# Split weights kept in device memory, the scan's chunks chained, and the rotary's GpSimd work moved, in a two-layer decoder trunk

## The chip, the cores and the metric

One core of a Trainium2 chip runs the whole kernel. The metric is the device time of one execution in microseconds (us); three runs of the kernel before gave a median of 2995.03 us (2994.13 to 2998.02). A core has five engines that run side by side: PE (matrix multiply, with PEld for its weight loads), DVE (VectorE), ACT (ScalarE), POOL (GpSimd) and SP (SyncE), which here issues the DMAs. Each engine takes its instructions in order. Tiles live in SBUF (128 partitions) and, for results of PE, in the banks of PSUM; tensors too large for that live in device memory (DRAM).

## What is computed

2048 tokens of width 1024, with 16 learned meta tokens ahead of them (2064 in all), pass two layers in float32. Each layer is h + norm(mixer(norm(h))).

```
layer 0:  q, k, v, g_a, glu_in, g_b = split(h @ w_in)            # 1024 -> 2816 = 22 blocks of 128
          a = sliding_window_attention(rope(q), rope(k), v, sinks) * silu(g_a)   # 8 heads, window 128, meta tokens always seen
          u = glu_in[:512] * sigmoid(glu_in[512:])
          c = silu(layer_norm(depthwise_conv31(u))) @ w_pw2 * silu(g_b)
          y = concat(a, c) @ w_out
layer 1:  q, k, v, g = split(h @ w_in)                            # 1024 -> 4096, 16 heads of 64
          z = q k^T / 8                                           # only keys before the query
          a = sigmoid(z) * product of sigmoid(-z) over the keys between it and the query   # stick-breaking, no softmax
          y = ((a @ v) * silu(g)) @ w_out
rope(x):  (x1 * cos - x2 * sin, x2 * cos + x1 * sin) on the two halves of a head
```

## The kernel before

*Precision.* PE multiplies in a reduced float format (`F32R`). To keep float32 accuracy, most operands are split into a high part (the value rounded to that format) and a low part (the rest), and a product is made of three matmuls, high x high, low x high and high x low (`mm3`, L126 to L130).

*Layer 0, first stage* (`stage1`, L251). The tokens are cut into 4 chunks (528 tokens, then three of 512). For a chunk, the normalised and transposed input stands in SBUF as a high and a low tile. `proj(m, ...)` (L277) multiplies it with block `m` of the 22 blocks of `w_in`: `weights` (L112) loads 512 KB by DMA into `raw` (two buffers), ACT casts it to the high part `wh` (L119) and POOL subtracts to get the low part `wl` (L120). Both parts have two buffers each, in a pool that the pointwise convolution's weights use too. The load carries a priority that lets the planner put it 60 instructions ahead. All 22 blocks are loaded and split again in each of the four chunks. The projections feed the rotary embedding (`rope`, L329: five per chunk), values, gates and the gated convolution input.

*The rotary.* ACT copies a projection out of PSUM (`qr`), four small DMAs make a copy with the halves exchanged (`qs`). Some time later, after the next projection (`turn`, L337 to L344), DVE multiplies `qr` by the cosines, POOL `qs` by the signed sines, DVE adds, POOL rounds to the high part and POOL subtracts for the low part; DMAs store both.

*The convolution* has 31 taps on DVE, one `scalar_tensor_tensor` of 128x512 each (L294), queued in the background and issued six at a time after projections. *The second stage* of layer 0 (`stage2`: attention over the window, layer norm, the pointwise product `pw` at L524, which loads and splits two weight blocks for each pair of token tiles) is interleaved with the first stage of the next chunk. The softmax's meta columns are copied by POOL into `pmc` (L447). The output projection of layer 0 runs into the start of layer 1.

*Layer 1.* For each of 8 pairs of heads, and in two halves of the queries, the projections of the next pair (`proj` at L736) are interleaved with attention (`attn`, L822). There, `chunk` (L882) works on two blocks of 128 queries, two heads, and up to 512 keys, from the latest keys back: PE makes the scores `z`, ACT makes `om` = sigmoid(-z) and `be` = sigmoid(z) from them (L902, L903), and on the diagonal POOL puts 1 and 0 where the key isn't before the query (L906). DVE then runs a product scan over `om` from the last key to the first (L910), started with the product of all chunks before it, and multiplies `be` with the scan's value one place on (L913). The product so far passes from chunk to chunk through POOL: it copies the scan's first column to `carry` (L912) and, for the next chunk, `carry` into the column behind the scan (L909); the first chunk has a 1 there (L907). PE transposes `be` (L930), ACT copies it out (L936), and PE multiplies it with the values (L944).

*Order.* The order of the instructions on each engine, and on SP's DMA queue, is made by a planner that simulates a timeline from the written order, priorities and its own costs; waits between engines are semaphores that it sets. A tile's buffer is given out anew when all that used it are through.

Of the kernel before, what the change touches and what calls it, by code (L numbers as in the profile page):

```python
# [10 lines left out]
F32 = mybir.dt.float32  # L11
F32R = mybir.dt.float32r
I32 = mybir.dt.int32
AF = mybir.ActivationFunctionType
ALU = mybir.AluOpType
# [3 lines left out]
P = 128  # L19
D = 1024  # L20
KB = D // P
SEQ = 2048
NM = 16
# [14 lines left out]
WP = 60  # L38
# [40 lines left out]
class Trunk:  # L79
# [29 lines left out]
        self.nc.gpsimd.tensor_scalar(hi, src, 1.0, 0.0, ALU.mult, ALU.add)  # L109
        self.nc.vector.tensor_tensor(lo, src, hi, ALU.subtract)  # L110

    def weights(self, pool, src, rpool, tag):  # L112
        nc = self.nc
        raw = rpool.tile([P, KB, P], F32, tag=tag, name="raw", bufs=2 if tag == "raw" else 1)
        wh = pool.tile([P, KB, P], F32R, tag="wh", name="wh")
        wl = pool.tile([P, KB, P], F32R, tag="wl", name="wl")
        with self.tc.high_priority(offset=WP):
            self.wdma = nc.sync.dma_start(raw, src).ins
        nc.scalar.copy(wh, raw)  # L119
        nc.gpsimd.tensor_tensor(wl, raw, wh, ALU.subtract)  # L120
        return wh, wl

    def mv(self, out, src):
# [54 lines left out]
    def layer0(self, after=None):  # L178
        tc, nc, a = self.tc, self.nc, self.a
        HALO = CW - 1  # L180
        qd = self.dram("q0d", [P, 2, 4, T], F32R)
        kd = self.dram("k0d", [2, 2, HD, T], F32R)
# [6 lines left out]
        c0, w2, w3 = (self.pool(left, n, b, side="left") for n, b in (("c0", 1), ("w2", 2), ("w3", 3)))  # L189
# [5 lines left out]
        pww = self.pool(left, "pww", 2, side="left")  # L195
# [3 lines left out]
        s1c, s1, s3 = (self.pool(early, n, b, side="right") for n, b in (("s1c", 1), ("s1", 2), ("s3", 2)))  # L199
# [51 lines left out]
        def stage1(c):  # L251
            tiles, base, TC = chunk(c)
# [4 lines left out]
            st = {}  # L257
# [17 lines left out]
            steps.append((0.0, start))  # L275

            def proj(m, evac):  # L277
                wh, wl = self.weights(pww, a["w_in0"][m], s1, "raw")
                turns = late[:]
                late.clear()  # L280
                for s0, sn in subs:
                    ps = self.bank(next(banks), "pj")
                    for k in range(KB):
                        self.mm3(ps[:, :sn], wh[:, k], wl[:, k], st["h"][:, k, s0 : s0 + sn], st["l"][:, k, s0 : s0 + sn], k == 0, k == KB - 1)
                    evac(ps[:, :sn], s0, sn)
                for f in turns:
                    f()
# [41 lines left out]
            def rope(m, put):  # L329
                qr = s1.tile([P, 528], F32, tag="qr", name="qr", bufs=3)  # L330
                qs = s1.tile([P, 528], F32, tag="qs", name="qs")
                proj(m, lambda ps, s0, sn: nc.scalar.copy(qr[:, s0 : s0 + sn], ps))
                for b in range(4):
                    nc.sync.dma_start(qs[b * 32 : b * 32 + 32, :TC], qr[(b ^ 1) * 32 : (b ^ 1) * 32 + 32, :TC])
                run_bg(CB)

                def turn():  # L337
                    nc.vector.tensor_tensor(qr[:, :TC], qr[:, :TC], st["ctab"][:, :TC], ALU.mult)
                    nc.gpsimd.tensor_tensor(qs[:, :TC], qs[:, :TC], st["stab"][:, :TC], ALU.mult)
                    nc.vector.tensor_tensor(qr[:, :TC], qr[:, :TC], qs[:, :TC], ALU.add)  # L340
                    hi, lo = qs[:, :TC].bitcast(F32R), qr[:, :TC].bitcast(F32R)
                    nc.gpsimd.tensor_scalar(hi, qr[:, :TC], 1.0, 0.0, ALU.mult, ALU.add)
                    nc.gpsimd.tensor_tensor(lo, qr[:, :TC], hi, ALU.subtract)
                    put(qs, qr)  # L344

                late.append(turn)
# [54 lines left out]
        def swa(t):  # L401
            n, o = toks(t), tok0(t)
# [29 lines left out]
            def soft():  # L432
                p, mx = S["p"], S["mx"]
                l = w2.tile([P, 8], F32, tag="l", name="l")
                nm = w2.tile([P, 8], F32, tag="nm", name="nm")
                es = w2.tile([P, 8], F32, tag="es", name="es")
                nc.vector.scalar_tensor_tensor(nm[:n], mx[:n], -0.125, nsink[:n], ALU.mult, ALU.min)
                nc.vector.tensor_tensor(es[:n], nm[:n], nsink[:n], ALU.subtract)
                nc.scalar.activation(es[:n], es[:n], AF.Exp)
                for hh in range(8):  # L440
                    nc.scalar.activation(p[:n, hh, :nk], p[:n, hh, :nk], AF.Exp, bias=nm[:n, hh : hh + 1], scale=0.125, accum_out=l[:n, hh : hh + 1])
                nc.vector.tensor_tensor(l[:n], l[:n], es[:n], ALU.add)
                nc.vector.reciprocal(l[:n], l[:n])
                S["pmc"] = pmc = w2.tile([P, 8, NM], F32, tag="pmc", name="pmc")
                for hh in range(8):
                    nc.vector.tensor_scalar(p[:n, hh, :nk], p[:n, hh, :nk], l[:n, hh : hh + 1], None, ALU.mult)  # L446
                nc.gpsimd.tensor_scalar(pmc[:n], p[:n, :, :NM], 1.0, 0.0, ALU.mult, ALU.add)  # L447

            def values():
                p, pmc = S["p"], S["pmc"]  # L450
# [28 lines left out]
        def cbranch(ut):  # L479
# [44 lines left out]
            def pw():  # L524
                ch, cl = S["ch"], S["cl"]
                gb = w2.tile([P, 4, 272], F32, tag="gb", name="gb", bufs=1)
                nc.sync.dma_start(gb[:, :, :N], gbd[:, :, b0 : b0 + N].rearrange("r p t -> p r t"))
                for m in range(4):
                    if m % 2 == 0:
                        wh, wl = self.weights(pww, a["w_pw2"][m // 2], w2, "yl")  # L530
                    ps = self.bank("pj", "pw")
                    for k in range(4):
                        kk = 4 * (m % 2) + k
                        self.mm3(ps[:, :N], wh[:, kk], wl[:, kk], ch[:, k, :N], cl[:, k, :N], k == 0, k == 3)
                    tt = w2.tile([P, 272], F32, tag="ctt", name="mc")
                    nc.vector.tensor_tensor(tt[:, :N], ps[:, :N], gb[:, m, :N], ALU.mult)
                    nc.sync.dma_start(md[4 + m, :, b0 : b0 + N], tt[:, :N])
# [271 lines left out]
    def layer1(self):  # L809
        tc, nc, a = self.tc, self.nc, self.a  # L810
# [11 lines left out]
        def attn(p, hf):  # L822
# [53 lines left out]
            def pair_steps(m):  # L876
                es = edges(2 * m + 2)
                steps.append((0.0, lambda: qload(m)))
                carry = c1.tile([P, 4], F32, tag="carry", name="carry", bufs=2) if len(es) > 1 else None
                qc0 = (2 * m % 4) * P  # L880

                def chunk(ei):  # L882
# [7 lines left out]
                    for h in range(2):  # L890
                        for x in range(2):
                            n = nbs[x] * P + mo
                            if n == 0:
                                continue
                            ci = carry[:, 2 * h + x : 2 * h + x + 1] if carry is not None else None
                            z = self.bank("pz", "z")
                            for i in range(2):
                                nc.tensor.matmul(z[:, :n], S["q"][2 * h + i][:, x * P : x * P + P], S["k"][h][:, k0 : k0 + n], start=(i == 0), stop=(i == 1))  # L898
                            om = w3.tile([P, 512], F32, tag="om", name="om")
                            be = w2.tile([P, 512], F32, tag=f"be{h}{x}", name="be")  # L900
                            P_ = w3.tile([P, 513], F32, tag="S", name="S")
                            nc.scalar.activation(om[:, :n], z[:, :n], AF.Sigmoid, scale=-0.125)  # L902
                            nc.scalar.activation(be[:, :n], z[:, :n], AF.Sigmoid, scale=0.125)  # L903
                            if first:
                                for tt, fill in ((om, 1.0), (be, 0.0)):
                                    nc.gpsimd.affine_select(tt[:, n - P : n], tt[:, n - P : n], [[-1, P]], ALU.is_gt, fill, base=0, channel_multiplier=1)  # L906
                                nc.gpsimd.memset(P_[:, n : n + 1], 1.0)  # L907
                            else:
                                nc.gpsimd.tensor_scalar(P_[:, n : n + 1], ci, 1.0, 0.0, ALU.mult, ALU.add)  # L909
                            nc.vector.tensor_tensor_scan(P_[:, :n][:, ::-1], om[:, :n][:, ::-1], om[:, :n][:, ::-1], P_[:, n : n + 1], ALU.mult, ALU.bypass)  # L910
                            if not last:
                                nc.gpsimd.tensor_scalar(ci, P_[:, 0:1], 1.0, 0.0, ALU.mult, ALU.add)  # L912
                            nc.vector.tensor_tensor(be[:, :n], be[:, :n], P_[:, 1 : n + 1], ALU.mult)  # L913
                            if last:
                                nc.gpsimd.tensor_scalar(S["am"][:, 2 * m % 4 + x, h], be[:, :NM], 1.0, 0.0, ALU.mult, ALU.add)
                            bes[h, x] = be
# [203 lines left out]
```

## Time and profile before

| | |
|---|---|
| median of three runs | 2995.03 us |
| profiled execution: its time, its span | 2996.4 us, 2994.7 us |
| mean granted PE clock | 0.970 |
| busy share of the span: PE, PEld, DVE, ACT, POOL | 92%, 74%, 79%, 51%, 50% |
| moved by DMA | 395.77 MB, mean 132 GB/s |

Rows of the profile read so. A group has line, engine, operation, what it writes and reads, shape and count; then busy us in all and mean ns of one; then the engine's idle time just before these instructions and what ended it. A wait has who waited, for whom, us in all, times, longest. A table of stretches has for each stretch its length, then busy us (and count) of PE, PEld, DVE, ACT, POOL, the granted PE clock, the share of the DMA engines and GB/s. The chain of waits goes back from the last instruction through whatever released each step. Matmuls are pipelined, so that a busy PE isn't always one at its peak.

### The profile page before, as it was taken

To read this page: it belongs to the slowest core of one execution; us is meant where nothing else is said; L and a number is where in the kernel's file an instruction comes from. 1 tells how busy PE (TensorE), PEld (TensorE's weight loads), DVE (VectorE), ACT (ScalarE), POOL (GpSimd) and SP (SyncE) were. 2 spreads that over 40 slices of the span, in tenths; PEclk is the share of its full clock that TensorE was granted. 3 is DMA by queue.
4 is the path that set the end of the run, shared out by engine and by line. 5 is a ranking of instruction groups with operands and counts; after the bars stand their busy time and mean duration, and the time that the engine had idled before them with its cause. 6 is when DMAs were issued, how large, how long until landed. Compare 5 with 4: busy or idle time off the path is not lost.

```text
span 2994.7 us, 49703 instructions
## 1 busy us (share of the span) xinstructions
PE 2761.3 (92%) x16110; PEld 2211.2 (74%) x16110; DVE 2358.1 (79%) x3656; ACT 1518.2 (51%) x3607; POOL 1483.4 (50%) x2580
## 2 busy tenths in 40 slices
PE   7788897887899999999999899999999999989998
PEld 6776676676668789888888677777777767766776
DVE  7989989989977683566667888788787888887874
ACT  4224343433455532455544566676676666755551
POOL 4645546455421122354445766565565566665430
PEclk9889898998999999999999999999999999999999
DMA  4445555455476566344445554234242332344322
GB/s 160 141 133 148 154 166 142 148 163 147 137 203 199 175 219 183 116 131 133 132 134 171 168 137 119 86 86 114 68 111 64 100 100 72 92 121 127 106 96 88
DMA packets 285556, 395.77 MB, mean 132 GB/s; under 512 B 44593, under 2 KB 198593, under 8 KB 282225
## 3 DMA queue, kind: packets, MB, share of 16 engines
q1 hardware_dynamic: 285296, 392.59, 44.4%
q8 instruction: 129, 2.11, 0.3%
q14 instruction: 131, 1.07, 0.1%
HBM read 270.21 MB, written 116.97 MB: 129 GB/s over the span
## 4 chain that ended last, share of the span: by engine, by line
PE 60%; DVE 21%; issue 6%; POOL 5%; ACT 4%; DMA 3%; SPq 1%; DVEq 0%; POOLq 0%; ACTq 0%
DVE y L294 11%; PE pj L128 8%; PE pj L129 8%; PE pj L130 8%; PE z L898 7%; PE av L944 7%; PE pt L930 7%; PE po L128 4%; PE po L130 4%; PE po L129 3%; DVE S L910 2%; ACT om L902 1%; DMA raw<-in_w_in 1%; DVE p L446 1%; ACT be L903 1%
## 5 line engine op out<-in xcount | busy, mean ns | idle before, releaser
L910 DVE TENSOR_TENSOR_SCAN S<-om,S 128x384 f32<-128x384 f32 (+5 forms) x768 | 744.2, 988 | 150.3 <-POOL om L906 67.7
L294 DVE SCALAR_TENSOR_TENSOR y<-u,cw,y 128x512 f32<-128x512 f32 (+1 forms) x480 | 515.4, 1079 | 7.3
L902 ACT ACTIVATE om<-z 128x384 f32<-128x384 f32 (+5 forms) x768 | 379.3, 512 | 209.5 <-PE z L898 135.2
L128 PE MATMUL pj<-th,wh 128*128 128x512 f32 (+2 forms) x1280 | 460.7, 360 | 8.0 <-POOL wh L109 4.5
L913 DVE TENSOR_TENSOR be<-be,S 128x384 f32<-128x384 f32 (+5 forms) x768 | 403.0, 549 | 72.7 <-ACT be L903 33.8
L130 PE MATMUL pj<-th,wl 128*128 128x512 f32 (+2 forms) x1280 | 452.4, 353 | 0.3 <-DVE wl L110 0.3
L129 PE MATMUL pj<-tl,wh 128*128 128x512 f32 (+2 forms) x1280 | 451.2, 352 | 0.0
L936 ACT COPY aT<-pt 128x512 f32<-128x512 f32 (+2 forms) x672 | 334.8, 505 | 201.2 <-PE pt L930 157.0
L898 PE MATMUL z<-kst,qt 128*128 128x384 f32 (+6 forms) x1536 | 396.4, 358 | 28.1 <-ACT be L903 26.9
L903 ACT ACTIVATE be<-z 128x384 f32<-128x384 f32 (+5 forms) x768 | 375.9, 506 | 76.5 <-PE pt L930 75.8
L930 PE MATMUL pt<-ident,be 128*128 128x128 f32 x2176 | 363.3, 281 | 24.3 <-ACT aT L936 9.7
L120 POOL TENSOR_TENSOR wl<-raw,wh 128x1024 fp32r<-128x1024 f32 x104 | 273.4, 2631 | 177.1 <-ACT wh L119 176.9
L912 POOL TENSOR_SCALAR carry<-S 128x1 f32<-128x1 f32 x512 | 265.8, 521 | 184.8 <-DVE S L910 160.3
L130 PE MATMUL pj<-hTh,wl 128*128 128x512 f32 (+2 forms) x880 | 321.7, 368 | 25.3 <-POOL wl L120 25.3
L930 PEld LDWEIGHTS pt<-ident,be 128*128 128x128 f32 x2176 | 252.7, 141 | 120.5 <-ACT aT L936 35.1
L128 PE MATMUL pj<-hTh,wh 128*128 128x512 f32 (+2 forms) x880 | 325.8, 371 | 12.3 <-DVE gt L366 6.4
L909 POOL TENSOR_SCALAR S<-carry 128x1 f32<-128x1 f32 x512 | 263.6, 517 | 136.6 <-DVE be L913 116.5
L129 PE MATMUL pj<-hTl,wh 128*128 128x512 f32 (+2 forms) x880 | 322.6, 367 | 1.3 <-DVE hTl L176 1.3
L898 PEld LDWEIGHTS z<-kst,qt 128*128 128x128 f32 x1536 | 249.0, 191 | 72.6 <-ACT be L903 51.9
L944 PE MATMUL av<-aT,vt 128*64 128x256 f32 (+1 forms) x2304 | 282.1, 381 | 4.6 <-DVE og L962 4.6
L128 PEld LDWEIGHTS pj<-th,wh 128*128 128x128 f32 x1280 | 241.8, 189 | 35.0 <-POOL wh L109 4.9
L130 PEld LDWEIGHTS pj<-th,wl 128*128 128x128 f32 x1280 | 240.9, 188 | 30.0 <-DVE wl L110 0.6
(177 smaller groups left out, 4817.4 us busy)
## 6 DMA issues: line engine op xcount, KB each, us to landing
raw<-in_w_in SPq DMA_DIRECT2D x164, 512.0 KB, 3.7
qt<-qhd SPq DMA_DIRECT2D x256, 64.0 KB, 2.6
qt<-qld SPq DMA_DIRECT2D x256, 64.0 KB, 2.4
kst<-khd SPq DMA_DIRECT2D x16, 516.0 KB, 7.8
kst<-kld SPq DMA_DIRECT2D x16, 516.0 KB, 10.0
qT<-q0d SPq DMA_DIRECT2D x32, 256.0 KB, 3.6
raw<-in_w_pw SPq DMA_DIRECT2D x16, 512.0 KB, 3.9
rawo<-in_w_out SPq DMA_DIRECT2D x16, 512.0 KB, 4.5
```

The source lines that it names most:

```text
L128: mm(out, sh, mh, start=first, stop=False)
L129: mm(out, sh, ml, start=False, stop=False)
L130: mm(out, sl, mh, start=False, stop=last)
L294: return lambda: nc.vector.scalar_tensor_tensor(y[:, :TC], u[:, w : w + TC], cw[:, j, w : w + 1], y[:, :TC], ALU.mult, ALU.add)
L898: nc.tensor.matmul(z[:, :n], S["q"][2 * h + i][:, x * P : x * P + P], S["k"][h][:, k0 : k0 + n], start=(i == 0), stop=(i == 1))
L902: nc.scalar.activation(om[:, :n], z[:, :n], AF.Sigmoid, scale=-0.125)
L903: nc.scalar.activation(be[:, :n], z[:, :n], AF.Sigmoid, scale=0.125)
L910: nc.vector.tensor_tensor_scan(P_[:, :n][:, ::-1], om[:, :n][:, ::-1], om[:, :n][:, ::-1], P_[:, n : n + 1], ALU.mult, ALU.bypass)
L913: nc.vector.tensor_tensor(be[:, :n], be[:, :n], P_[:, 1 : n + 1], ALU.mult)
L930: nc.tensor.transpose(pt[:, o : o + P], bes[h, x][:, mo + b * P : mo + b * P + P], self.ident)
L936: cps.append(nc.scalar.copy(aT[:, lo:hi], pt[:, lo:hi]))
L944: mi = nc.tensor.matmul(av[h * HD : h * HD + HD, qc0 + x0 : qc0 + 256], S["v"][:, b0 + b, h * HD : h * HD + HD], at, start=not S["started" ...
```

## The change

Three things, on the same arithmetic.

1. *Weights.* `weights` gets a name under which the split halves are kept. The first time, it loads, casts and subtracts as before and then stores both halves to device memory (two DMAs of 512 KB). Each later time it loads the two halves straight into `wh` and `wl`; no `raw` tile, no cast, no subtraction. There are 22 + 2 first times and 66 + 14 later ones.
2. *Rotary and softmax.* The sine product and the low part go from POOL to DVE, the rounding from POOL to ACT; the `pmc` copy goes from POOL to ACT.
3. *Scan.* `om` and `be` get one column more, into which POOL writes a 1 each time (behind `om`'s keys, before `be`'s first). The scan runs over that column too and starts from the value it is given: 1, or the leading column of the product of the chunk before. As that column of `be` is 1, the product there is the scan's value, which is what the next chunk starts from. `carry` and its two POOL copies, and the memset of the scan's start, are gone.

```diff
-    def weights(self, pool, src, rpool, tag):
+    def weights(self, pool, src, rpool, tag, kept):
         nc = self.nc
+        if kept in self.drams:
+            wh = pool.tile([P, KB, P], F32R, tag="wh", name="wh")
+            wl = pool.tile([P, KB, P], F32R, tag="wl", name="wl")
+            with self.tc.high_priority(offset=WP):
+                for i, w in enumerate((wh, wl)):
+                    self.mv(w, self.drams[kept][:, i])
+            return wh, wl
+        kd = self.dram(kept, [P, 2, KB, P], F32R)
         raw = rpool.tile([P, KB, P], F32, tag=tag, name="raw", bufs=2 if tag == "raw" else 1)
...
         nc.gpsimd.tensor_tensor(wl, raw, wh, ALU.subtract)
+        for i, w in enumerate((wh, wl)):
+            self.mv(kd[:, i], w)
         return wh, wl
...
-                wh, wl = self.weights(pww, a["w_in0"][m], s1, "raw")
+                wh, wl = self.weights(pww, a["w_in0"][m], s1, "raw", f"wk{m}")
...
-                    nc.gpsimd.tensor_tensor(qs[:, :TC], qs[:, :TC], st["stab"][:, :TC], ALU.mult)
+                    nc.vector.tensor_tensor(qs[:, :TC], qs[:, :TC], st["stab"][:, :TC], ALU.mult)
                     nc.vector.tensor_tensor(qr[:, :TC], qr[:, :TC], qs[:, :TC], ALU.add)
                     hi, lo = qs[:, :TC].bitcast(F32R), qr[:, :TC].bitcast(F32R)
-                    nc.gpsimd.tensor_scalar(hi, qr[:, :TC], 1.0, 0.0, ALU.mult, ALU.add)
-                    nc.gpsimd.tensor_tensor(lo, qr[:, :TC], hi, ALU.subtract)
+                    nc.scalar.copy(hi, qr[:, :TC])
+                    nc.vector.tensor_tensor(lo, qr[:, :TC], hi, ALU.subtract)
...
-                nc.gpsimd.tensor_scalar(pmc[:n], p[:n, :, :NM], 1.0, 0.0, ALU.mult, ALU.add)
+                nc.scalar.copy(pmc[:n], p[:n, :, :NM])
...
-                        wh, wl = self.weights(pww, a["w_pw2"][m // 2], w2, "yl")
+                        wh, wl = self.weights(pww, a["w_pw2"][m // 2], w2, "yl", f"wp{m // 2}")
...
-                carry = c1.tile([P, 4], F32, tag="carry", name="carry", bufs=2) if len(es) > 1 else None
+                lead = {}
...
-                            om = w3.tile([P, 512], F32, tag="om", name="om")
-                            be = w2.tile([P, 512], F32, tag=f"be{h}{x}", name="be")
+                            om = w3.tile([P, 513], F32, tag="om", name="om")
+                            bl = w2.tile([P, 513], F32, tag=f"be{h}{x}", name="be")
+                            be = bl[:, 1:]
+                            nc.gpsimd.memset(om[:, n : n + 1], 1.0)
+                            nc.gpsimd.memset(bl[:, 0:1], 1.0)
...
-                                nc.gpsimd.memset(P_[:, n : n + 1], 1.0)
-                            else:
-                                nc.gpsimd.tensor_scalar(P_[:, n : n + 1], ci, 1.0, 0.0, ALU.mult, ALU.add)
-                            nc.vector.tensor_tensor_scan(P_[:, :n][:, ::-1], om[:, :n][:, ::-1], om[:, :n][:, ::-1], P_[:, n : n + 1], ALU.mult, ALU.bypass)
-                            if not last:
-                                nc.gpsimd.tensor_scalar(ci, P_[:, 0:1], 1.0, 0.0, ALU.mult, ALU.add)
-                            nc.vector.tensor_tensor(be[:, :n], be[:, :n], P_[:, 1 : n + 1], ALU.mult)
+                            init = lead[h, x] if (h, x) in lead else 1.0
+                            nc.vector.tensor_tensor_scan(P_[:, : n + 1][:, ::-1], om[:, : n + 1][:, ::-1], om[:, : n + 1][:, ::-1], init, ALU.mult, ALU.bypass)
+                            nc.vector.tensor_tensor(bl[:, : n + 1], bl[:, : n + 1], P_[:, : n + 1], ALU.mult)
+                            lead[h, x] = bl[:, 0:1]
```

More of the change, by code (lines that the diff above doesn't have):

```diff
@@ L894, in chunk @@
                                 continue
-                            ci = carry[:, 2 * h + x : 2 * h + x + 1] if carry is not None else None
                             z = self.bank("pz", "z")
```

## Prediction, made before the changed kernel ran

> **What bounds the kernel now.** I read the table of stretches first, to see which engine is full where; then the chain of waits inside a stretch; then the groups and single instructions on that chain. The table (times from the span's start, busy us and count of each engine, granted clock, DMA share, GB/s):
>
> ```profile
> 0.00:210.00 210.00, 161.78 (x1163) 155.23 (x1163) 186.96 (x215) 63.86 (x110) 114.27 (x99) 0.94 0.44 138
> 210.00:860.00 650.00, 553.34 (x2633) 433.35 (x2633) 597.29 (x987) 265.72 (x562) 324.50 (x278) 0.92 0.54 157
> 860.00:1130.00 270.00, 261.74 (x1389) 216.53 (x1388) 201.47 (x505) 139.40 (x276) 46.62 (x51) 0.98 0.66 196
> 1130.00:1650.00 520.00, 512.07 (x3527) 446.05 (x3526) 302.08 (x479) 234.65 (x693) 230.02 (x593) 1.00 0.48 142
> 1650.00:2790.00 1140.00, 1082.58 (x6433) 808.96 (x6433) 939.85 (x1249) 734.34 (x1799) 716.99 (x1461) 0.99 0.36 104
> ```
>
> The columns after the length are PE, PEld, DVE, ACT, POOL. From 860 us on PE is full (262 of 270, 512 of 520, 1083 of 1140). Before that it isn't: DVE has 597 of 650 us and PE 553, at a granted clock of 0.92. So the kernel has two halves with different limits. The chain in 0 to 860 us, and for comparison in 1900 to 2600 us:
>
> ```profile
> by line: DVE y L294 38.8%; issue 10.0%; PE pj L128 3.3%; PE pj L129 3.3%; PE pj L130 3.0%; DVE p L446 3.0%; DVE p L430 2.2%; POOL wl L120 2.2%; DVE qr L338 2.0%; POOL rs_t L92 1.6%; DVE gt L366 1.6%; DVE qr L340 1.6%; DVE yn L505 1.5%; POOL
> ...
> by line: PE z L898 15.8%; PE pt L930 13.5%; PE av L944 13.5%; PE pj L128 11.4%; PE pj L129 11.4%; PE pj L130 11.3%; issue 5.6%; DVE S L910 4.3%; ACT om L902 2.9%; ACT be L903 1.6%; PE av L960 1.4%; DVE be L913 1.2%; POOL om L906 1.0%; ACT a
> ```
>
> Layer 0 hangs on the convolution's taps (L294), layer 1 on PE. Why the taps cost what they do is seen in their spread (min/median/max) and in one of them beside its neighbour on POOL:
>
> ```profile
> L294 DVE SCALAR_TENSOR_TENSOR y<-u,cw,y x480: 699/752/3007, 38.4 to 836.5; 128x512 f32<-128x512 f32 x120, 128x528 f32<-128x528 f32 x40
> ...
> 303.93 2.96 DVE L294 SCALAR_TENSOR_TENSOR y<-u,cw,y 128x512 f32<-128x512 f32 x1
> ...
> 303.99 2.35 POOL L120 TENSOR_TENSOR wl<-raw,wh 128x1024 fp32r<-128x1024 f32 x1
> ```
>
> A tap that takes 0.75 us took 2.96 us, the 2.35 us of the weight subtraction on POOL longer. The two engines block each other.
>
> **The change, part by part.** (a) *POOL's long instructions leave layer 0.* All in 0 to 860 us:
>
> ```profile
> L294 DVE SCALAR_TENSOR_TENSOR y<-u,cw,y 128x512 f32<-128x512 f32 (+1 forms) x480 | 515.4, 1079 | 7.3
> ...
> L120 POOL TENSOR_TENSOR wl<-raw,wh 128x1024 fp32r<-128x1024 f32 x98 | 259.0, 2645 | 163.9 <-ACT wh L119 163.7
> L339 POOL TENSOR_TENSOR qs<-qs,stab 128x512 f32<-128x512 f32 (+1 forms) x20 | 33.7, 1684 | 35.1 <-DMA qs<-qr 31.1 <-PE pt_v L354 2.2 <-PE pj L130 1.0
> L343 POOL TENSOR_TENSOR qr<-qr,qs 128x512 fp32r<-128x512 f32 (+1 forms) x20 | 32.0, 1602 | 1.4
> L342 POOL TENSOR_SCALAR qs<-qr 128x512 fp32r<-128x512 f32 (+1 forms) x20 | 19.5, 974 | 43.5 <-DVE qr L340 43.5
> ```
>
> Had every tap its median, they would take 480 x 0.752 = 361 us; 515.4 - 361 = 154 us are blocked time. Of the four POOL groups' 344 us, 24 of the 98 subtractions stay (22 blocks of the first chunk and two of the pointwise weights). 74/98 x 259.0 = 196 us go, and the rotary's 85: 281 of 344, or 0.82. So 0.82 x 154 = 126 us leave DVE. It gains two instructions for each of 20 rotary blocks. Their nearest rows are
>
> ```profile
> L338 DVE TENSOR_TENSOR qr<-qr,ctab 128x512 f32<-128x512 f32 (+1 forms) x20 | 19.9, 996 | 1.5 <-DMA qs<-qr 1.5
> L340 DVE TENSOR_TENSOR qr<-qr,qs 128x512 f32<-128x512 f32 (+1 forms) x20 | 18.1, 905 | 0.0
> ```
>
> means that hold blocked time as well; I take the tap's 0.75 us (between 0.70 and 1.0): 40 x 0.75 = 30. DVE loses 96 us of work. The chain holds 0.388 x 860 = 334 us of the taps' 515, or 0.65 of them, so I let 0.65 pass: **-62 us** (0 if PE takes over at once, -126 if all passes and the rotary hides).
>
> (b) *Weights loaded ready-made.* L120 stands on the chain with 0.022 x 860 = 19 us; three quarters go: **-14 us**. In exchange, 80 times (66 projection blocks, 14 pointwise) two 512 KB loads replace one, and what they land in is free only when the projection two back is through: the raw tile had been loaded ahead, the finished halves can't be. The cast's row, landing times (issues, KB, median us), and PE's pace:
>
> ```profile
> L119 ACT CAST wh<-raw 128x1024 fp32r<-128x1024 f32 x104 | 109.0, 1049 | 275.3 <-PE pj L129 139.7 <-issue 37.9 <-DMA raw<-in_w_in 36.8
> ...
> raw<-in_w_in SPq DMA_DIRECT2D x164, 512.0 KB, 3.7
> kst<-kld SPq DMA_DIRECT2D x16, 516.0 KB, 10.0
> ...
> 312.57 0.40 PE L128 MATMUL pj<-hTh,wh 128*128 128x512 f32 x1
> 312.81 0.40 PE L129 MATMUL pj<-hTl,wh 128*128 128x512 f32 x1
> ```
>
> One load lands in 3.7 us; four that are issued together (two of each half for two heads) in 10.0. Two lie between; I take 6.5 and 0.5 for the second issue. A projection of 24 matmuls at 0.235 us takes 5.6, so in a dense run of projections the weights are 7.0 - 5.6 = 1.4 us late, where the cast and the subtraction (1.05 and 2.6 us) were in time. If half of the 74 run dense that is 52 us of PE's time; where DVE is behind, and it is on 0.65 of the chain, it costs nothing: 0.35 x 52 = **+18 us** (0, all hidden, to 74 x 1.4 = +104, cover gone). The DMA engines carry it: 157 GB/s at a share of 0.54, and 70 times 0.52 MB more in 600 us makes about 225 GB/s, a share near 0.8.
>
> The Trainium skill ("SBUF — State Buffer", The DMA setup-cost knee) fits a transfer as 2 us and its bytes at 436 GB/s: 4.4 us for both halves as an estimate, nothing late, and the sum would be 18 us lower. For one half it gives 3.2 us where this trace has 3.7, so I stay with the rows.
>
> (c) *Stores in the first chunk.* 24 times two 512 KB, 25 MB, of which 23 fall into the first 210 us, beside 29 MB at 0.44 (138 GB/s): a share near 0.8. They are queued on SP behind ACT's cast and POOL's subtraction, and the tile isn't written again before its store is through; matmuls of 5.6 us cover most of it. **+4 us** (0 to 22 x 1.4 = 31).
>
> (d) *ACT in the rotary and the softmax.* ACT gets 20 copies and 17 small ones and loses 80 casts:
>
> ```profile
> L447 POOL TENSOR_SCALAR pmc<-p 128x128 f32<-128x128 f32 (+1 forms) x17 | 12.9, 756 | 98.7 <-DVE p L446 95.5 <-DVE mv L488 3.2
> ```
>
> It has the time (266 of 650 us). But its copy now waits for DVE as L342 did (43.5 us in all), PSUM evacuations queue behind it, and DVE's subtraction waits for ACT. **+4 us** (0 to 44).
>
> (e) *The scan.* In layer 1 these leave POOL:
>
> ```profile
> L912 POOL TENSOR_SCALAR carry<-S 128x1 f32<-128x1 f32 x512 | 265.8, 521 | 184.8 <-DVE S L910 160.3 <-DVE rs_m L88 2.3
> L909 POOL TENSOR_SCALAR S<-carry 128x1 f32<-128x1 f32 x512 | 263.6, 517 | 136.6 <-DVE be L913 116.5 <-DVE rstd L93 0.6
> L907 POOL MEMSET S<- 128x1 f32 x256 | 24.2, 95 | 8.6 <-issue 8.0 <-DVE be L913 0.3
> L910 DVE TENSOR_TENSOR_SCAN S<-om,S 128x384 f32<-128x384 f32 (+5 forms) x768 | 744.2, 988 | 150.3 <-POOL om L906 67.7 <-ACT om L902 65.0 <-POOL S L909 5.7
> ```
>
> 554 us go, 1536 memsets at 95 ns (146 us) come. They are hidden behind PE, and would have to free PE to count. DVE's scan waited for L909 5.7 us only. What PE waits for in 1130 to 2790 us is ACT:
>
> ```profile
> PEld z L898 <- ACT be L903: 51.9, 103, 2.9
> PEld pt L930 <- ACT aT L936: 35.1, 101, 2.7
> ```
>
> The added waits: a memset waits until the scan or the transposes have left its tile; the causal selects (L906) and weight splits (L109) queue behind it on POOL, and the scan behind those. The scan also has one column more, 1 in 384, and its start is now a product that DVE itself made. PE's whole gap in the two stretches is 65 us. I take **-10 us** (-25 to +33). The upper end comes from PE, which now reads the transposes' operand one element off:
>
> ```profile
> L930 PE MATMUL pt<-ident,be 128*128 128x128 f32 x2176 | 363.3, 281 | 24.3 <-ACT aT L936 9.7 <-ACT ev L784 9.6 <-DVE be L913 1.6
> L783 PE MATMUL ptv<-ident,ev 128*128 128x128 f32 (+1 forms) x136 | 37.9, 296 | 0.1
> ```
>
> Two kinds of transposes differ by 15 ns (281 and 296), and 2176 x 15 ns is 33 us.
>
> Sum: -62 - 14 + 18 + 4 + 4 - 10 = -60. The profiled execution took 2996.4 us (span 2994.7), 1.4 above the median of the runs, 2995.0; so **2935 us** for the median.
>
> **Rivals.** *PE warms up (0.22).* Between 210 and 860 us PE's clock was 0.92, where it is dense 1.00. If DVE's waits go, its 553 us shrink to 509; DVE's share of the cut (96 less some 20 for the first chunk) leaves it 520. At 95% full, as PE is in 1650 to 2790, the stretch takes 540 to 550 us: -105, with -10 from layer 1 and some from the first chunk 2875. Against it: two engines this evenly loaded seldom both stay full. The Trainium skill ("TensorE: Matmul & The Clock Gate", HAM oscillation) has this rule: idle gaps over about 3.4 us drop the clock; the 0.92 agrees, and weights that come 1.4 us late wouldn't trip it.
>
> *The weights wait in SP's queue (0.13, slower).* SP issues in order, and a load can now stand behind a store that waits for DVE:
>
> ```profile
> SPq L369 <- DVE gt L366: 71.0, 15, 9.0
> SPq L298 <- DVE y L294: 20.5, 7, 10.5
> SPq L413 <- DVE mt L474: 15.9, 4, 5.9
> ```
>
> In 210 to 860 us the first is 4.7 us each time, and the three are 107 of 650 us. A load in six late by 4.7 us, on top of 1.4 for all: 2.2 us each, 145 for 66. PE's 553 + 145 = 698 us is over 650: +48, and with -10 from layer 1 about 3035. It decides from (650 - 553)/66 = 1.5 us late on each. Against it: these stores wait less when DVE isn't blocked, and the loads are given priority.
>
> *Hidden anyway (0.10).* DVE's freed time is eaten by late weights alone; layer 0 stays, layer 1 gives a few us or takes them: 2992. Small changes of order in layer 1 belong here.
>
> **How the numbers follow.** The forecast has 0.55, its own range 2900 to 2970. Holding 8 in 10, the range reaches into the warm case and the hidden one: 2865 to 3000. Under 0.2%, 6 us, a measurement of this kernel can't tell. Faster: 0.55 + 0.22 and a little of the hidden case, 0.79; same 0.07; slower 0.14.
>
> **What would show it.** (a): the taps' mean falls from 1079 to near 830 ns and 210 to 860 us shrinks by some 60. If the taps fall and the stretch doesn't, the weights are late: PE's waits before L128 or L130 in projections then name the loads of the kept halves. (c): the first chunk's end stays near 210 us. (e): POOL's busy time after 1130 us falls by 400 us, PE's hardly moves, and the step from one pair of heads to the next, which the chain shows in two places,
>
> ```profile
> 2172.47 2.28 DVE S L910 x3
> 2302.35 2.28 DVE S L910 x3
> ```
>
> stays at 130 us. The prediction is wrong altogether if layer 1 moves by more than layer 0.

## The result, and the profile after

The changed kernel takes 2909.35 us (median of 4 runs, 2907.3 to 2916.46) beside 2994.58 for the kernel before on the same chip: a ratio of 0.972, 95% interval 0.9699 to 0.974, 85 us faster. The forecast was 2935, 60 us faster, with a range of 2865 to 3000. Its profiled execution took 2916.46 us (span 2914.7), 80 less than the one of before.

Where the 80 us went is seen in the first and last start of two groups: the taps, which end the first stage of layer 0, and the gated output of each four query blocks in layer 1 (L962 before, L971 after). Before, then after; the numbers are min/median/max in ns, first and last start in us.

```profile
L294 DVE SCALAR_TENSOR_TENSOR y<-u,cw,y x480: 699/752/3007, 38.4 to 836.5; 128x512 f32<-128x512 f32 x120, 128x528 f32<-128x528 f32 x40
L962 DVE TENSOR_TENSOR og<-av,g x32: 657/680/692, 1234.1 to 2931.5; 128x512 f32<-128x512 f32 x32
```

```profile
L304 DVE SCALAR_TENSOR_TENSOR y<-u,cw,y x480: 716/752/2975, 37.5 to 761.9; 128x512 f32<-128x512 f32 x120, 128x528 f32<-128x528 f32 x40
L971 DVE TENSOR_TENSOR og<-av,g x32: 656/682/693, 1160.8 to 2851.8; 128x512 f32<-128x512 f32 x32
```

The taps end 74.6 us earlier, the first output of layer 1 starts 73.3 us earlier, and from the first to the last output it is 1691.0 us where it was 1697.4. So layer 0's first stage gave 75 us, the stretch between the layers nothing, and layer 1 gave 6. Of the 75, 10.5 had come by the end of the first chunk: its last convolution result was stored at 203.2 us, where it was 213.7. The table of stretches after (columns as in the prediction; a row of the same times covers later work than before):

```profile
0.00:210.00 210.00, 168.08 (x1200) 159.71 (x1201) 183.32 (x261) 66.25 (x130) 88.20 (x83) 0.94 0.77 263
210.00:860.00 650.00, 598.91 (x2948) 467.02 (x2947) 511.87 (x1127) 250.24 (x581) 66.09 (x147) 0.96 0.80 240
...
1130.00:1650.00 520.00, 505.05 (x3442) 430.05 (x3441) 344.15 (x531) 259.92 (x756) 213.84 (x774) 0.99 0.47 140
1650.00:2790.00 1140.00, 1093.71 (x6483) 818.72 (x6482) 940.40 (x1264) 737.12 (x1776) 354.50 (x1559) 0.99 0.35 100
```

In 210 to 860 us DVE has fallen from 597 to 512 us and POOL from 325 to 66. PE has risen from 553 to 599 with 315 more matmuls, its clock from 0.92 to 0.96, and DMA from 0.54 to 0.80. The groups behind it, of the whole span:

```profile
L304 DVE SCALAR_TENSOR_TENSOR y<-u,cw,y 128x512 f32<-128x512 f32 (+1 forms) x480 | 392.1, 822 | 8.0
L349 DVE TENSOR_TENSOR qs<-qs,stab 128x512 f32<-128x512 f32 (+1 forms) x20 | 13.8, 688 | 0.0
L353 DVE TENSOR_TENSOR qr<-qr,qs 128x512 fp32r<-128x512 f32 (+1 forms) x20 | 13.8, 688 | 0.1
...
L911 POOL MEMSET om<- 128x1 f32 x768 | 74.6, 99 | 768.9 <-DVE S L920 753.9 <-DVE rstd L93 6.5 <-DVE rs_m L88 4.5
L912 POOL MEMSET be<- 128x1 f32 x768 | 64.1, 99 | 113.4 <-PE pt L939 109.9 <-issue 0.4 <-POOL am L924 0.2
L939 PE MATMUL pt<-ident,be 128*128 128x128 f32 x2176 | 361.4, 280 | 17.8 <-ACT ev L794 6.2 <-ACT aT L945 6.0 <-DVE be L921 2.2
```

A tap takes 822 ns instead of 1079 on the mean; the two instructions that DVE took over from POOL in the rotary take 28 us together. What took DVE's place stands in the chain of 0 to 760 us and in PE's waits there:

```profile
by line: DVE y L304 12.3%; DMA wl<-wk 11.3%; PE pj L140 11.1%; PE pj L139 10.5%; PE pj L138 10.5%; issue 3.8%; DMA md<-mc 3.3%; DMA qs<-qr 2.3%; DMA qT<-q0d 2.0%; DMA wh<-wk 2.0%; SPq L134 1.8%; PE pt_p L474 1.8%; SPq L344 1.6%; PE s L439 1
...
PE pj L138 <- DMA wh<-wk: 18.7, 9, 5.0
PE pj L140 <- DMA wl<-wk: 14.7, 15, 4.3
```

The taps have 12.3% of the chain, where they had 38.8%; the loads of the kept low halves now have 11.3% of it.

### The profile page after: what moved, and what is told of

It is laid out like the page before. It is cut to its first block, busy times and chain, and to the rows that moved or that the text cites. A ratio compares the mean times of both kernels' runs of the same rounds, so it can differ in the third digit from the quotient of the medians.

```text
span 2914.7 us, 49596 instructions
## 1 busy us (share of the span) xinstructions
PE 2742.9 (94%) x16110; PEld 2191.9 (75%) x16110; DVE 2214.4 (76%) x3696; ACT 1463.5 (50%) x3568; POOL 775.3 (27%) x2679
## 4 chain that ended last, share of the span: by engine, by line
PE 68%; DVE 10%; DMA 9%; issue 5%; ACT 3%; POOL 2%; SPq 2%; DVEq 0%; ACTq 0%; POOLq 0%
PE pj L140 10%; PE pj L138 10%; PE pj L139 10%; PE z L907 7%; PE av L953 7%; PE pt L939 6%; PE po L138 4%; PE po L140 4%; PE po L139 4%; DVE y L304 3%; DMA wl<-wk 3%; DVE S L920 2%; DMA raw<-in_w_in 1%; DVE be L921 1%; DMA md<-mc 1%
## 5 line engine op out<-in xcount | busy, mean ns | idle before, releaser
L920 DVE TENSOR_TENSOR_SCAN S<-om,be 128x401 f32<-128x401 f32 (+3 forms) x512 | 536.3, 1068 | 72.4 <-ACT om L914 51.7
L921 DVE TENSOR_TENSOR be<-be,S 128x385 f32<-128x385 f32 (+5 forms) x768 | 413.8, 563 | 76.2 <-POOL be L912 21.8
L304 DVE SCALAR_TENSOR_TENSOR y<-u,cw,y 128x512 f32<-128x512 f32 (+1 forms) x480 | 392.1, 822 | 8.0
L911 POOL MEMSET om<- 128x1 f32 x768 | 74.6, 99 | 768.9 <-DVE S L920 753.9
L139 PEld LDWEIGHTS pj<-tl,wh 128*128 128x128 f32 x1280 | 241.4, 189 | 25.1 <-issue 0.4
L920 DVE TENSOR_TENSOR_SCAN S<-om 128x257 f32<-128x257 f32 (+4 forms) x256 | 204.6, 811 | 62.8 <-POOL om L918 49.9
```

The costliest lines, as they stand in the source:

```text
L139: mm(out, sh, ml, start=False, stop=False)
L304: return lambda: nc.vector.scalar_tensor_tensor(y[:, :TC], u[:, w : w + TC], cw[:, j, w : w + 1], y[:, :TC], ALU.mult, ALU.add)
L920: nc.vector.tensor_tensor_scan(P_[:, : n + 1][:, ::-1], om[:, : n + 1][:, ::-1], om[:, : n + 1][:, ::-1], init, ALU.mult, ALU.bypass)
L921: nc.vector.tensor_tensor(bl[:, : n + 1], bl[:, : n + 1], P_[:, : n + 1], ALU.mult)
```

## The experiments

Two theories were set against each other. The prediction's: what counts is that POOL's long instructions stop blocking DVE. The rival: the way of the weights (load, cast, subtraction) was itself on the chain, and it became shorter. All times are medians beside runs of the kernel before on the same chip (2993.0 to 2995.6).

### One part at a time

*The kept weights alone.*

```diff
-                wh, wl = self.weights(pww, a["w_in0"][m], s1, "raw")
+                wh, wl = self.weights(pww, a["w_in0"][m], s1, "raw", f"wk{m}")   # weights() and w_pw2 as in the change; rotary, pmc, scan as before
```

> Only the kept weights are added to the kernel before; rotary, softmax copy and scan as before. Theory 1 (blocking: what counts is that POOL's long subtractions no longer stop DVE): 196 of the 281 us of removed POOL work go here, so the taps' mean falls from 1079 to about 895 ns (0.70 of the measured fall of 257), and 55 to 65 of the 85 us come: 2930 to 2940 us. Theory 2 (the weights' own path matters: load, cast and subtraction stood on the chain of waits): almost all of the 85 us come here, about 2915, with the taps' mean playing no part. If the two parts only work together, as each alone leaves DVE blocked, 2960 or more.

Measured 2945.9 us, ratio 0.9843 (0.9822 to 0.9863): 48 us faster. That is 6 us outside the range of theory 1, on its slow side, and far from the 2915 of theory 2. The taps' mean fell to 886 ns, where theory 1 had 895.

*The rotary and the softmax's copy alone.*

```diff
-                    nc.gpsimd.tensor_tensor(qs[:, :TC], qs[:, :TC], st["stab"][:, :TC], ALU.mult)
+                    nc.vector.tensor_tensor(qs[:, :TC], qs[:, :TC], st["stab"][:, :TC], ALU.mult)
...
-                    nc.gpsimd.tensor_scalar(hi, qr[:, :TC], 1.0, 0.0, ALU.mult, ALU.add)
-                    nc.gpsimd.tensor_tensor(lo, qr[:, :TC], hi, ALU.subtract)
+                    nc.scalar.copy(hi, qr[:, :TC])
+                    nc.vector.tensor_tensor(lo, qr[:, :TC], hi, ALU.subtract)
```

> Only the rotary's three POOL instructions and the softmax's small copy are moved to DVE and ACT; weights and scan as before. Theory 1 (blocking): 85 of 344 us of POOL's long work go, 38 us of blocked time, and DVE gains 40 x 0.69 = 28 us of work: net 5 to 10 us faster, 2985 to 2990. Rival (the rotary's hand-offs between DVE and POOL were themselves what the first chunk waited for; it ended 11 us earlier where the prediction had it 4 later): 15 to 25 us faster, with most of it in the first 210 us.

Measured 2970.56 us, ratio 0.9919 (0.9904 to 0.9934): 23 us faster. That is the size of the rival and not of theory 1, but not in the rival's place: the last convolution result of the first chunk was stored 4 us earlier (209.4 us, before 213.7), and the last tap started 23 us earlier (813.6, before 836.5). The tap groups of the two kernels (weights alone, then rotary alone):

```profile
L304 DVE SCALAR_TENSOR_TENSOR y<-u,cw,y 128x512 f32<-128x512 f32 (+1 forms) x480 | 425.0, 886 | 9.4
```

```profile
L294 DVE SCALAR_TENSOR_TENSOR y<-u,cw,y 128x512 f32<-128x512 f32 (+1 forms) x480 | 466.9, 985 | 5.2
L339 DVE TENSOR_TENSOR qs<-qs,stab 128x512 f32<-128x512 f32 (+1 forms) x20 | 13.8, 688 | 0.0
L343 DVE TENSOR_TENSOR qr<-qr,qs 128x512 fp32r<-128x512 f32 (+1 forms) x20 | 13.8, 688 | 2.4 <-ACT qs L342 2.4
```

The rotary's 85 us on POOL had cost the taps 515.4 - 466.9 = 48.5 us, not the 38 of an equal share; less 27.6 us of new work that is 21 us, about the 23 that were gained. But the taps aren't all that DVE does. These are the rows of the stretch up to the last tap, before, with the weights alone and with the rotary alone:

```profile
0.00:836.00 836.00, 694.39 (x3683) 576.87 (x3683) 770.05 (x1164) 315.67 (x642) 433.83 (x363) 0.92 0.50 148
...
0.00:788.00 788.00, 684.99 (x3668) 564.77 (x3669) 647.04 (x1162) 251.14 (x573) 234.76 (x290) 0.95 0.77 238
...
0.00:813.00 813.00, 692.36 (x3703) 572.39 (x3703) 754.98 (x1206) 331.98 (x679) 356.32 (x291) 0.93 0.51 152
```

With the rotary alone DVE's work fell by 15 us (770 to 755), since some other instructions of it took longer (the softmax's scaling 52.1 us, before 49.0; the product in the convolution's silu 19.2, before 13.1). That is less than the 23 gained, so DVE's relief alone doesn't explain the rotary. PE also waited less for POOL's weight subtractions (12.7 us up to 860 us, before 25.3), which is one candidate for the rest; this isn't shown. With the weights alone DVE lost 123 us of work, 90 of them on the taps, and the time fell by 48.

*The scan alone* (the diff of `pair_steps` and `chunk` in layer 1, nothing else).

> Only the scan's chaining is changed; layer 0 as before. In the trace of the whole change layer 1 gave 6 us (first to last gated output 1697 us against 1691). Theory 1: layer 1 is held by PE, so 5 to 8 us, 2987 to 2990, and POOL's busy time falls by about 410 us with no more effect. Rival: the 6 us come from another order of the instructions or from PE's clock and not from the scan: no change, 2995.

Measured 2990.17 us over 11 runs, ratio 0.9987 (0.9978 to 0.9996): 4 us faster, just clear of no change and a little less than theory 1 had. POOL's busy time fell by 407 us (1483.4 to 1076.3, from the first part of its page) with no more effect than this:

```profile
PE 2763.4 (92%) x16110; PEld 2212.7 (74%) x16110; DVE 2361.3 (79%) x3656; ACT 1519.3 (51%) x3607; POOL 1076.3 (36%) x2836
```

The three parts alone sum to 48 + 23 + 4 = 75 us of the 85.

### Is it blocking? POOL's work put back

```diff
                 for i, w in enumerate((wh, wl)):
                     self.mv(w, self.drams[kept][:, i])
+            if tag == "raw":
+                spare = rpool.tile([P, KB, P], F32, tag=tag, name="raw", bufs=2)
+                nc.gpsimd.tensor_tensor(spare, wh.bitcast(F32), wl.bitcast(F32), ALU.subtract)   # pool_reads
+                # pool_writes has instead: for _ in range(3): nc.gpsimd.memset(spare, 0.0)
             return wh, wl
```

> The changed kernel, and after each of the 66 later loads of projection weights POOL again subtracts the two loaded halves into the spare raw tile, which nothing reads: POOL's old work at its old place, with the new way of getting the weights. Theory 1 (blocking is the cause): taps go back from 822 ns to about 950, layer 0 loses most of what the kept weights gave (48 us when they came alone), so 30 to 60 us slower than the changed kernel's 2909: 2940 to 2970. Theory 2 (the gain is the shorter way of the weights): no more than a few us, 2910 to 2915.

> As the run before, but POOL fills the spare tile three times with zeros instead: POOL busy for about as long, writing only and reading nothing. If what blocks DVE is any long POOL instruction, 2940 to 2970 like the run with reads. If it is POOL's reading of SBUF, the taps stay at 822 ns and the time at 2909 to 2915.

Measured: with reads 2968.53 us (0.9919, 0.9902 to 0.9936), 59 us above the changed kernel; with writes 2922.12 (0.9765, 0.9748 to 0.9781), 13 us above it. Groups of the two kernels:

```profile
L307 DVE SCALAR_TENSOR_TENSOR y<-u,cw,y 128x512 f32<-128x512 f32 (+1 forms) x480 | 470.5, 986 | 7.9
L122 POOL TENSOR_TENSOR raw<-wh,wl 128x1024 f32<-128x1024 f32 x66 | 168.8, 2558 | 271.3 <-DMA wl<-wk 264.5 <-DMA qs<-qr 6.7
```

```profile
L308 DVE SCALAR_TENSOR_TENSOR y<-u,cw,y 128x512 f32<-128x512 f32 (+1 forms) x480 | 395.6, 830 | 7.6
L123 POOL MEMSET raw<- 128x1024 f32 x198 | 183.7, 971 | 0.5
```

169 us of POOL that nothing waits for (the trace has no wait for them), but that reads SBUF, add 78 us to the taps and 59 to the time; 184 us that only write add 3.5 us to the taps. That is the blocking, with the new way of the weights left as it is: theory 2 would have had no more than a few us. The 13 us of the second run seem to have a reason of their own. Its memsets wait for no load and bunched up in 210 to 420 us, and what they slow there isn't the taps. DVE in that stretch and the stretch's row, writes first, the changed kernel second:

```profile
L308 DVE SCALAR_TENSOR_TENSOR y<-u,cw,y 128x512 f32<-128x512 f32 x120 | 91.8, 770 | 1.6
L460 DVE TENSOR_SCALAR p<-p,l 128x272 f32<-128x272 f32 x32 | 26.2, 882 | 0.0
L305 DVE TENSOR_SCALAR y<-u,cw,cv 128x512 f32<-128x512 f32 x4 | 10.0, 2497 | 0.1
...
210.00:420.00 210.00, 182.20 (x855) 141.74 (x854) 187.60 (x353) 74.86 (x181) 177.48 (x220) 0.93 0.75 227
```

```profile
L304 DVE SCALAR_TENSOR_TENSOR y<-u,cw,y 128x512 f32<-128x512 f32 x133 | 99.0, 753 | 1.7
L456 DVE TENSOR_SCALAR p<-p,l 128x272 f32<-128x272 f32 x32 | 9.0, 351 | 0.0
L301 DVE TENSOR_SCALAR y<-u,cw,cv 128x512 f32<-128x512 f32 x4 | 2.2, 548 | 0.0
...
210.00:420.00 210.00, 190.77 (x908) 150.00 (x907) 165.55 (x365) 75.52 (x182) 35.03 (x64) 0.95 0.80 238
```

The instructions with one tensor input more than doubled (the softmax's scaling of 128x272 from 351 to 882 ns, the convolution's first tap from 548 to 2497), some 25 to 30 us in all, and the ones with two hardly changed. So a POOL instruction that only writes does block DVE, but other instructions of it. PE got through 53 matmuls fewer in this stretch (855 against 908); that this made the 13 us is argued from there.

### What the kept weights cost

```diff
         if kept in self.drams:
-            wh = pool.tile([P, KB, P], F32R, tag="wh", name="wh")
-            wl = pool.tile([P, KB, P], F32R, tag="wl", name="wl")
+            self.turn = getattr(self, "turn", 0) + (tag == "raw")
+            if tag == "raw" and self.turn % 3 == 0:
+                wh, wl = (rpool.tile([P, KB, P], F32R, tag=tag, name=n, bufs=2) for n in ("wh", "wl"))
+            else:
+                ...
```

> The changed kernel, but every third projection block of the later chunks lands in the two raw tiles, which stand empty there, so that weights have three places instead of two and can be loaded a projection ahead. The prediction's term for late weights was 18 us on the chain (52 us of PE's time). If that is right, 10 to 20 us faster than 2909: 2890 to 2900. Rival: DMA, at a share of 0.80 in these chunks, or DVE is what now holds layer 0, and an earlier request lands no earlier: 2905 to 2912.

Measured 2898.36 us (0.9683, 0.9666 to 0.9699), 11 us below the changed kernel. PE's waits for the same loads are now

```profile
PE pj L144 <- DMA wl<-wk: 7.4, 6, 3.6
...
PE pj L142 <- DMA wh<-wk: 5.8, 5, 2.2
...
210.00:760.00 550.00, 513.56 (x2576) 406.66 (x2575) 461.95 (x994) 223.23 (x516) 68.81 (x148) 0.97 0.83 253
```

They come to 13 us instead of 33, at a DMA share of 0.83 in 210 to 760 us, where the changed kernel has 0.80. The lateness was real, and smaller than the whole 11% that the chain gives to these loads.

```diff
-        for i, w in enumerate((wh, wl)):
-            self.mv(kd[:, i], w)
+        if kept == one:                       # no_stores: "wk0", "wp0"; later chunks load that block
+            for i, w in enumerate((wh, wl)):
+                self.mv(kd[:, i], w)
...
-                    self.mv(w, self.drams[kept][:, i])
+                    self.mv(w, self.drams[kept[:2] + "0"][:, i])     # one_place: this line alone, all stores kept
```

> The changed kernel with one block's halves stored instead of 24: the later chunks load that one block every time. So the projections of later chunks use the wrong weights, and 48 stores less 4 are left out; all durations are as before. It measures the prediction's term for the stores, 4 us (0 to 31): 2905. Rival (the first chunk was 10 us shorter though it stored 23 MB more, so the stores are hidden whole): 2909, no change.

> The changed kernel with all its stores, but the later chunks load the halves of one block every time (so their projections use the wrong weights; durations as before). With one block stored and loaded the time was 2898, 11 us below the changed kernel, though the first chunk was no shorter. If the stores cost these 11 us (they are still under way, or ahead in the queue, when the second chunk's loads begin): 2907 to 2912 here. If it was reading the same 1 MB again and again that made the loads quicker: 2896 to 2900.

Measured 2898.44 us (0.9683, 0.9668 to 0.9697) without the stores, and 2909.51 (0.9722, 0.9709 to 0.9734) with all stores and one place to load from. So leaving out the stores is worth 11 us, and where the loads read from costs nothing. Where the 11 us arise isn't settled. The first chunk, in which the stores run, ended no earlier without them (its last convolution result was stored at 205.8 us, in the changed kernel at 203.2). What is shorter is the later chunks' wait for the kept loads: 20 us of PE's time (11.0 and 8.6), in the changed kernel 33, though the last store of the first chunk was issued at 187 us, before these chunks. The planner makes another order without the stores, and whether that order is the reason isn't shown. Since a third place shortens the same waits, the two times 11 us may overlap.

### The subtractions that were left

```diff
-        nc.gpsimd.tensor_tensor(wl, raw, wh, ALU.subtract)
+        nc.vector.tensor_tensor(wl, raw, wh, ALU.subtract)   # dve_split: this alone; three_buffers_dve: with the three places; dve_split_all: without kept weights
```

> The changed kernel with the 24 subtractions that are left on POOL done by DVE. In the first chunk taps still lose 34 us to them, and PE waits 15 us for them; DVE would do them in 24 x 1.22 = 29 us. Theory (blocking): about even in DVE's work, with a shorter way for PE: 3 to 10 us faster, 2900 to 2906. Rival: DVE's order puts the subtraction behind taps and PE waits longer: 2910 to 2920.

> Three places for the weights (11 us faster alone) and the 24 first subtractions on DVE. If both act, in different chunks, their gains add: 2890 to 2896. If the first chunk doesn't gain, 2898.

> The changed kernel without kept weights: every one of the 104 weight blocks is loaded, cast and split again, but DVE subtracts and not POOL. No blocked time is left, no DMA is added, and DVE has 80 x 1.22 = 98 us more than where the kept weights and DVE's first subtractions stand together (2886). If the gain is POOL off DVE's back and nothing more, and DVE is the bound again: 2886 plus 0.6 to 1.0 of 98, 2945 to 2985. If the loads of the kept halves (DMA at a share of 0.80, weights late) cost nearly as much as these subtractions, 2900 to 2930: keeping the weights would then bring little of its own.

Measured: 2885.68 us (0.9642, 0.9628 to 0.9656); with three places 2874.84 (0.9597, 0.9583 to 0.9611), which is the fastest kernel of this study, 35 us below the changed one, the sum of the two gains (24 and 11); without any kept weights 2895.59 (0.9674, 0.9657 to 0.9692).

The first gained 24 us where 3 to 10 were expected. Taps and first chunk in that kernel:

```profile
L304 DVE SCALAR_TENSOR_TENSOR y<-u,cw,y x480: 698/752/1403, 38.4 to 739.0; 128x512 f32<-128x512 f32 x119, 128x528 f32<-128x528 f32 x41
...
0.00:210.00 210.00, 181.77 (x1306) 169.93 (x1307) 175.99 (x316) 70.95 (x146) 36.42 (x61) 0.98 0.84 287
```

No tap is over 1.4 us, DVE's busy time fell by 21 us (2214.4 to 2193.7 in the first part of the pages) though it took on 29 us of subtractions, and PE got through 106 matmuls more in the first 210 us, at a clock of 0.98 instead of 0.94. DVE does in 1.2 us, in its own turn, what held a tap up for as much as 2.2 us (2975 - 752 ns) when POOL did it.

The last of the three was a miss of the expectation on the other side. All 104 subtractions on DVE, 80 more than in the first of these kernels, cost 10 us and not 59 to 99, and that kernel is 14 us faster than the changed one without keeping anything. Its stretch and groups:

```profile
210.00:860.00 650.00, 588.58 (x2920) 462.84 (x2920) 585.21 (x1220) 321.46 (x660) 97.13 (x159) 0.95 0.59 174
...
L294 DVE SCALAR_TENSOR_TENSOR y<-u,cw,y 128x512 f32<-128x512 f32 (+1 forms) x480 | 346.5, 748 | 0.7
L120 DVE TENSOR_TENSOR wl<-raw,wh 128x1024 fp32r<-128x1024 f32 x104 | 128.1, 1232 | 12.5 <-ACT wh L119 11.9 <-ACT pT L466 0.3
```

128 us of subtractions on DVE stand in for 273 us on POOL in the kernel before, DVE is at 585 of 650 us, PE at 589, and DMA stays at 0.59. So most of what the kept weights brought was POOL's absence; of their own, with DVE doing what is left, they bring 10 us with two places for the weights and 21 with three.

## Why the prediction was right, point by point

*What bounds it.* Right. DVE bound layer 0 by blocked time, and layer 1 hung on PE: of 80 us, 75 came from layer 0, 6 from layer 1.

*(a) Blocked time.* The mechanism was right, and so was the size for the taps: 480 x (1079 - 822) ns = 123 us left the taps where 126 were forecast, and the forecast of "near 830 ns" stands beside 822. The rotary's two products cost 27.6 us (30). The term that was mis-sized is the work that DVE loses. The prediction counted the taps alone and put nothing for DVE's other instructions: 96 us with the new work taken off. Up to the last tap DVE lost 140 us (770 before, 630 after; the row of before is with the parts above):

```profile
0.00:761.00 761.00, 674.82 (x3663) 557.05 (x3664) 629.59 (x1201) 267.27 (x607) 151.75 (x217) 0.96 0.79 246
```

The other instructions had been blocked too. The softmax's scaling and the scaling of the input, before and then after:

```profile
L446 DVE TENSOR_SCALAR p<-p,l 128x272 f32<-128x272 f32 (+2 forms) x136 | 49.0, 430 | 0.2
L246 DVE SCALAR_TENSOR_TENSOR xs<-xt,rstd,gpre 128x1024 f32<-128x1024 f32 (+1 forms) x13 | 29.4, 2260 | 9.1 <-POOL rstd L93 9.0
...
L456 DVE TENSOR_SCALAR p<-p,l 128x272 f32<-128x272 f32 (+2 forms) x136 | 37.0, 342 | 0.2
L256 DVE SCALAR_TENSOR_TENSOR xs<-xt,rstd,gpre 128x1024 f32<-128x1024 f32 (+1 forms) x13 | 20.8, 1601 | 6.1 <-POOL rstd L93 6.0
```

With 140 in the place of 96, the prediction's own sum gives -91 for (a) and -79 for layer 0, which gave 75. The share of 0.65 isn't refuted, but it isn't shown by itself either. Of the 140 us, 75 came out as time and 65 as waiting of DVE (its idle time up to the last tap grew from 66 to 131 us): 0.54, with the loads, the stores and POOL's own step on the chain still in it. Nor is it the same for each part: 48 of 123 us with the weights alone, 23 of 15 with the rotary alone.

*(b) Late weights.* The mechanism was right: a projection in a dense run waits for its loads, 33 us of PE's waits name them. Of the 18 us forecast a third place gave back 11. The forecast's landing time of 6.5 us for the pair was close:

```profile
wh<-wk SPq DMA_DIRECT2D x66, 512.0 KB, 5.2
wl<-wk SPq DMA_DIRECT2D x66, 512.0 KB, 6.1
```

One wait that was not forecast: with DMA at 0.80 the rotary's small exchange lands later (4.4 us after its issue instead of 2.0), and DVE waits for it, 21.4 us where it was 1.5. It comes with the kept weights (21.6 us with the weights alone, 0.9 with the rotary alone).

```profile
L348 DVE TENSOR_TENSOR qr<-qr,ctab 128x512 f32<-128x512 f32 (+1 forms) x20 | 13.9, 693 | 25.3 <-DMA qs<-qr 21.4 <-ACT vr L360 2.3 <-ACT vt L366 1.5
```

*(c) Stores.* 4 us forecast, 11 measured by leaving them out, inside its bounds of 0 to 31. The place was wrong: the first chunk, which the sign for (c) kept near 210 us, ended 10.5 us earlier with all its stores, and the 11 us don't show in it. *(d) ACT.* Its copy waited for DVE as POOL had, 42.3 us in all (43.5 before); what that cost wasn't measured by itself.

```profile
ACT qs L352 <- DVE qr L350: 42.3, 11, 7.8
```

*(e) The scan.* -10 forecast, 4 us faster by the scan alone and 6 in the trace of the whole; the step from one pair of heads to the next stayed at 130 us. POOL lost 407 us in the scan's run, as forecast (408). The operand off by one cost PE nothing: its transposes take 280 ns and took 281.

*The rivals.* The warm PE came halfway: the clock rose to 0.96, not 1.00, and the time lies between it (2875) and the forecast. The weights in SP's queue didn't decide: a projection's loads were late by far less than 1.5 us on the mean (33 us of waits over 66 is 0.5). Nothing was hidden anyway.

## What to carry to other kernels

Before work is taken away from a helper engine that shares SBUF with the busy one, look at the spread of the busy engine's instructions: a maximum four times the median, with the helper's instruction beside it, shows the price. Count it over all instructions of the busy engine and not over the most frequent alone (140 us here, not 96), and expect a part of it as time, since the engine then waits for others: 75 of 140 us with the whole change, 48 of 123 with the weights alone. The cheapest cure here was to give the helper's work to the busy engine itself (1.2 us of DVE for 2.6 of POOL); with that done, keeping results in device memory to avoid the work brought 10 us more, and 21 once its loads had a third place to land in.

## What was not expected of the hardware

POOL's memsets, which read nothing, left DVE's instructions with two tensor inputs alone (770 against 753 ns with POOL busy for 177 of 210 us) but made those with one tensor input and a per-partition factor two and a half to four and a half times as long (351 to 882 ns for 128x272, 548 to 2497 ns for 128x512). The Trainium skill ("SBUF — State Buffer", Who interferes with whom) says both: two SBUF inputs collide only with POOL instructions that read, and `tensor_scalar` can run in a mode that takes both ports and then collides with any POOL instruction that uses them. These rows agree, though the trace doesn't say which mode an instruction ran in; the expectation for that run had only thought of the first half.
